# Attention in a two-layer encoder trunk: own tiles for the rotation, and another order of squares, evictions and rotations

## The chip, the cores and the metric

The kernel runs on one core of a Trainium2 chip. The metric is device time in microseconds (us). Every number below comes from the page of one profiled execution, from views of its trace, or from the run times.

Engines in the profile: PE (TensorE; PEld is its loading of weights), DVE (VectorE), ACT (ScalarE), POOL (GpSimd) and SP (SyncE, which issues nearly all DMAs). Each engine executes its own list of instructions in order, and waits at an instruction until the semaphores of other engines allow it.

## The reference

A trunk of two layers on 256 tokens of 1024 channels. Each layer is half a SwiGLU feed-forward block, a mixer, and another half block; the first mixer is a convolution module, the second is latent attention. All in float32. The change lies in the attention:

```python
def mla(h, positions, w_a, g_q, g_kv, w_uq, w_ukv, w_o):
    a = h @ w_a                                   # 512 query, 256 key/value, 64 rotary columns
    c_q = rmsnorm(a[..., :Q_LORA], g_q)
    c_kv = rmsnorm(a[..., Q_LORA:Q_LORA + KV_LORA], g_kv)
    k_rope = a[..., Q_LORA + KV_LORA:]
    q = jnp.einsum("bsc,chd->bshd", c_q, w_uq)    # 8 heads of 128 + 64
    q_nope, q_rope = q[..., :QK_NOPE], q[..., QK_NOPE:]
    kv = jnp.einsum("bsc,chd->bshd", c_kv, w_ukv)
    ...
    q_rope = apply_rope(q_rope, cos[:, :, None, :], sin[:, :, None, :])
    k_rope = apply_rope(k_rope, cos, sin)
    ...                                           # chunk-causal softmax, values, w_o
```

`h` is itself an rmsnorm of the stream, with gain `mix_norm`.

## The kernel before

**Splitting.** Float32 products are made of three passes (`mm3`, L267): both operands are split into a high part, rounded to the format that PE multiplies at full rate (`hi`, `Xh`, `CQh`), and a low part, the rest (`lo`, `Xl`, `CQl`). For weights, ACT casts the high part (L185) and DVE subtracts the low part (L186), each block of 128 x 2048 in two pieces of 1024. Blocks are loaded by SP into `raw` (3 buffers), their parts lie in `hi` and `lo` (5 buffers each). A `raw` buffer is free for the next load when its casts are done.

**Rows.** The 256 tokens are two row tiles of 128 (tb 0 and 1, the first and second rows).

**The stage around the change** (`mla_in`, L1104). For each row tile, `low` (L1124) makes the query product `a` (512 columns, weights wa 0 and 1) and then the key product `a` (320 columns, wa 2 and 3). `normed` (L1136) normalizes each: two squares on ACT with sums (`squares`, L293, each writes a scratch tile `junk` that nobody reads), sums and power -1/2 on POOL (`power`, L302), a product with the row's own factor `R[tb]` (L1139), and on DVE the scaled copy `cn` (L1141). The squares are scaled by `R[tb]`, so they need it too. `key_rope` (L1144) scales the 64 rotary key columns (`kx`) and rotates them twice (`rope`, L1085), into both halves of `kd`. PE then transposes `cn` (`tp`, L313), ACT evicts the high parts (L328) and DVE the low parts (L332), into `CQ` for queries and `CKh`, `CKl` for keys (`split_rows`, L321). The rotary queries `qr` (L1198) are the first product of `CQ`; each row tile is rotated on DVE into `qrope` (L1205). `nope` (L1180) makes the other queries and keys.

**The rotation** is three products and a sum on DVE: by the cosines (L1093), two halves by the sines (L1095), and their sum (L1097). The first product goes to `t1`, a tile of the pool `tmp` with tag "s", two buffers, which the scratch of the squares, `junk`, shares:

```python
        t1 = tmp.tile([P, 512], F32, tag="s", name=uid("rp1"))
        t2 = pool.tile([P, 512], F32, tag="rp", name=uid("rp2"), bufs=2)
```
```python
        junk = tmp.tile([P, 512], F32, tag="s", name=uid("junk"))
```

**The stream's own norm** (`Norm`, L356). The first rows are transposed by PE. The second rows of `h` go another way: DVE transposes blocks of 32, and two DMAs per half bring them to the right partitions (`turn_blocks`, L340, tiles `ht`, `hd`, `hb`). `end(q)` (L410) evicts half q of the second rows from `hb`: four `Xh` on ACT (L417), four `Xl` on DVE (L418), ordered behind the casts of the last loaded weight block. `late` (L424) does both halves and then `rms(1)`: the squares of `h` (ACT) and R of the second rows (POOL).

**What sets the order.** A scheduler orders each engine's list by priority and by its own estimate of times. Functions marked `urgent` (L191) get a high priority; `order(a, b)` (L135) puts a behind b; weight casts stand behind the last six urgent pieces of work of their engine (`behind`, L139). Before, in the first rows' key step, the whole of `X.late()` came ahead of the loads and the key norm:

```python
                if tb == 0 and i == 1:
                    X.late()
                    load_ahead(1)
```

Of the kernel before, what the change touches and what calls it, by code (L numbers as in the profile page):

```python
# [11 lines left out]
F32 = mybir.dt.float32  # L12
# [3 lines left out]
AF = mybir.ActivationFunctionType  # L16
ALU = mybir.AluOpType
AX = mybir.AxisListType

P = 128  # L20
# [11 lines left out]
H = 8  # L32
# [4 lines left out]
KVL = 256  # L37
# [25 lines left out]
GCOL = {}  # L63
# [19 lines left out]
def trunk(ctx: ExitStack, tc: tile.TileContext, x, xt, pos, invf, gains, gfin, wdw,  # L83
          f1w13, f1w2, f2w13, f2w2, cw1, cw2, wa, wuq, wukv, wo, wpair, out):
    nc = tc.nc
# [5 lines left out]
    tmp = ctx.enter_context(tc.tile_pool(name="tmp", bufs=2))  # L91
    small = ctx.enter_context(tc.tile_pool(name="small", bufs=4))
# [5 lines left out]
    def uid(s):  # L98
        n_uid[0] += 1
        return f"{s}_{n_uid[0]}"  # L100
# [29 lines left out]
    loaded = []  # L130
    n_used = [0]
# [3 lines left out]
    def order(ins, first):  # L135
        tc.add_manual_dep(ins.ins, first.name, mybir.DependencyInfo(
            mybir.DependencyClass.NoSync, mybir.DependencyReason.DATA), reason="order")
# [7 lines left out]
    casts = {}  # L145
# [140 lines left out]
    def rstd(src, n, name, scale_in=1.0, after=()):  # L286

        ss = small.tile([P, 2], F32, tag="ss", name=uid("ss"))
        for i in range(2):
            squares(ss, src, n, i, scale_in, after if i else ())  # L290
        return power(ss, n, name)

    def squares(ss, src, n, i, scale_in=1.0, after=()):  # L293
        nh = n // 2
        junk = tmp.tile([P, 512], F32, tag="s", name=uid("junk"))
        sq = nc.scalar.activation(junk[:, :nh], src[:, i * nh:(i + 1) * nh], AF.Square, scale=scale_in,  # L296
                                  accum_out=ss[:, i:i + 1])
        for a in after:
            order(sq, a.ins)
        return sq  # L300

    def power(ss, n, name):  # L302
        ms = small.tile([P, 2], F32, tag="ms", name=uid("ms"))
        nc.gpsimd.tensor_tensor(ms[:, 0:1], ss[:, 0:1], ss[:, 1:2], op=ALU.add)  # L304
        nc.gpsimd.tensor_scalar(ms[:, 1:2], ms[:, 0:1], 1.0 / n, EPS, op0=ALU.mult, op1=ALU.add)
        r = small.tile([P, 1], F32, tag="r", name=uid(name))
        nc.gpsimd.tensor_tensor(r, ms[:, 1:2], neghalf, op=ALU.pow)
        return r
# [11 lines left out]
    @urgent  # L320
    def split_rows(src, q, n, gcol, dh, dl, tb, after=(), low_after=(), turned=None,  # L321
                   lows=None):

        b = transposed(src, q, n, after, turned)
        for j in range(n):
            k = q + j
            g = G[:, gcol + k:gcol + k + 1]
            high = nc.scalar.activation(dh[:, k, tbs(tb)], b[:, j * P:(j + 1) * P], AF.Copy, scale=g)  # L328
        for j in range(n):
            k = q + j  # L330
            g = G[:, gcol + k:gcol + k + 1]
            low = nc.vector.scalar_tensor_tensor(dl[:, k, tbs(tb)], b[:, j * P:(j + 1) * P], g,  # L332
                                                 dh[:, k, tbs(tb)].bitcast(F32), op0=ALU.mult, op1=ALU.subtract)
            if lows is not None:
                lows.append(low)
            for a in low_after:
                order(low, a.ins)
        return high
# [17 lines left out]
    class Norm:  # L356


        def __init__(self, gname, half=False, turn_by_dma=None):
            self.col = GCOL[gname]  # L360
            self.half = half

            self.pool = turn_by_dma
            self.turning = []
            self.whole = False
            self.xh = xp.tile([P, KT, S], F32R, tag="Xh", name=uid("Xh"))
            self.xl = xp.tile([P, KT, S], F32R, tag="Xl", name=uid("Xl"))
            self.r = [None] * NT
            self.rh = [None] * NT
            self.turned = ()  # L370
            self.lows = []

            self.between = None

# [34 lines left out]
        @urgent  # L409
        def end(self, q):  # L410

            for j in range(4):
                k = 4 * q + j
                g = G[:, self.col + k:self.col + k + 1]
                t = self.turning[q][:, j]
                high, low = (x[:, k, tbs(1)].rearrange("p (i q) -> p i q", q=32) for x in (self.xh, self.xl))
                both = (nc.scalar.activation(high, t, AF.Copy, scale=g),  # L417
                        nc.vector.scalar_tensor_tensor(low, t, g, high.bitcast(F32), op0=ALU.mult, op1=ALU.subtract))  # L418

                for i in range(PIECES):  # L420
                    for ins, cast in zip(both, casts[len(loaded) - 1, i]):
                        order(ins, cast.ins)

        def late(self):  # L424

            if self.whole:
                return
            if self.pool:
                for q in range(2):
                    self.end(q)  # L430
            else:
                self.part(1, 1)
            self.rms(1)
# [648 lines left out]
        nc.scalar.activation(sn[:, :, 1, :], r3, AF.Sin)  # L1082
        return cc, sn

    def rope(pool, dst, src, n, cc, sn, tb):  # L1085

        w = n * 64
        t1 = tmp.tile([P, 512], F32, tag="s", name=uid("rp1"))
        t2 = pool.tile([P, 512], F32, tag="rp", name=uid("rp2"), bufs=2)
        a = t1[:, :w].rearrange("p (n i f) -> p n i f", i=2, f=32)  # L1090
        b = t2[:, :w].rearrange("p (n i f) -> p n i f", i=2, f=32)
        full = [P, n, 2, 32]
        nc.vector.tensor_tensor(a, src, cc[:, tb, :, :].unsqueeze(1).to_broadcast(full), op=ALU.mult)  # L1093
        for i in range(2):
            nc.vector.tensor_tensor(b[:, :, i, :], src[:, :, 1 - i, :],  # L1095
                                    sn[:, tb, i, :].unsqueeze(1).to_broadcast([P, n, 32]), op=ALU.mult)
        nc.vector.tensor_add(dst, t1[:, :w], t2[:, :w])  # L1097


# [4 lines left out]
    def mla_in(act, X, make_next, cc, sn):  # L1104
        R = X.r
        CQ = act.tile([P, H, S], F32R, tag="CQ", name="CQ")
        CQh, CQl = CQ[:, :4, :], CQ[:, 4:, :]
        CKh = act.tile([P, 2, S], F32R, tag="CKh", name="CKh")
        CKl = act.tile([P, 2, S], F32R, tag="CKl", name="CKl")
# [23 lines left out]
            return u  # L1133

        @urgent
        def normed(u, n, tb):  # L1136
            r2 = rstd(u[:, :n], n, "r2", scale_in=R[tb])
            rr = small.tile([P, 1], F32, tag="rr", name=uid("rr"))
            nc.gpsimd.tensor_tensor(rr, r2, R[tb], op=ALU.mult)  # L1139
            cn = act.tile([P, n], F32, tag=f"cn{n}", name=uid("cn"), bufs=2)  # L1140
            nc.vector.tensor_scalar(cn, u[:, :n], rr, None, op0=ALU.mult)  # L1141
            return cn

        def key_rope(u, tb):  # L1144
# [10 lines left out]
        cq, ck, kd = [], [], []  # L1155
        last = None
        for tb in range(NT):
            for i, w in enumerate((QL, KVL + ROPE)):
                u = low(parts[2 * i:2 * i + 2], w, tb, last)
                last = last_low[0]  # L1160
                if tb == 0 and i == 1:
                    X.late()
                    load_ahead(1)
                if i == 0:
                    cq.append(normed(u, QL, tb))
                    if tb == 1:
                        load_ahead()
                else:
                    ck.append(normed(u, KVL, tb))
                    kd.append(key_rope(u, tb))  # L1170
                if tb == 1 and i == 1:
                    split_rows(cq[0], 0, 4, GCOL["q"], CQh, CQl, 0)
# [22 lines left out]
        for tb in range(NT):  # L1195
            u = bank("A", "qr")
            for k in range(4):
                mm3(u, CQh[:, k, tbs(tb)], CQl[:, k, tbs(tb)], hi[:, k * 512:(k + 1) * 512],  # L1198
                    lo[:, k * 512:(k + 1) * 512], k == 0, k == 3)
            if tb == 0:  # L1200
                split_rows(cq[1], 0, 4, GCOL["q"], CQh, CQl, 1)
                for t in range(NT):
                    split_rows(ck[t], 0, 2, GCOL["kv"], CKh, CKl, t)
            q = act.tile([P, 512], F32, tag="cn512", name=uid("qrope"), bufs=2)
            rope(act, q, u.rearrange("p (n i f) -> p n i f", i=2, f=32), H, cc, sn, tb)  # L1205
            qr.append(q)
        part, = weights()
        nope(part, QN, 4, CQh, CQl, 512, 0, (0, 4))
        for t in range(NT):
            b = transposed(kd[t], 0, 1)  # L1210
# [3 lines left out]
        for tb in range(NT):  # L1214
            b = transposed(qr[tb], 0, 4)
# [4 lines left out]
        for tb in range(NT):  # L1220
            for d in range(2):
                b = bank("A", "v")
# [107 lines left out]
    X = mla(X, lambda act: Norm("ffn2_1", half=True, turn_by_dma=rows), cc, sn)  # L1330
# [96 lines left out]
```

## Time and profile before

| | |
|---|---|
| median of 3 runs | 933.79 us (932.66 to 934.49) |
| the profiled execution | 933.97 us, of which its span 932.2 us |
| mean granted clock of TensorE | 0.993 |
| SP's queue | 193.27 MB, 59.5% of 16 DMA engines' span |
| chain that ended last | PE 91%, DVE 4%, ACT 2%, DMA 1%, POOL 1%, issue 1% |

The profile's times count from the first instruction. A row of a timeline has start, duration, engine, line, operation, output and inputs, shapes and count, and in brackets the idle time before it with its releaser. A row of the waits has engine, line and tile, who was waited for, the total in us, the times and the longest. A row of the windows has, for each stretch, the busy time of PE, PEld, DVE, ACT and POOL, then the granted clock of TensorE, the DMA share and GB/s. The attention's preparation lies between 642 us, where PE starts `a`, and 698 us, where it starts the scores in earnest.

### The profile page before, as it was taken

Reading aid. Unit: us, or ns where it says so; the run is one execution under the profiler, and the core shown is the slowest. Engines: PE = TensorE matmul, PEld = TensorE weight load, DVE = VectorE, ACT = ScalarE, POOL = GpSimd, SP = SyncE. Lnnn points to the kernel's source line nnn. Section 1 sums busy time; section 2 is a strip of 40 time slices with the busy share of each in tenths; the row PEclk is TensorE's granted clock in tenths of the full one; section 3 lists DMA queues with packets and bytes.
Section 4 is the critical chain, followed back from the end, with each engine's and each line's share of the span. In section 5 each row is a group of like instructions: output and inputs, shape, how many; then the busy total and the mean of one; then the engine's idle time right before and its main releaser. Section 6 shows DMA issues by size and latency. Waiting matters only on the chain.

```text
span 932.2 us, 12108 instructions
## 1 busy us (share of the span) xinstructions
PE 914.9 (98%) x4346; PEld 767.0 (82%) x4346; DVE 590.1 (63%) x931; ACT 494.8 (53%) x844; POOL 123.4 (13%) x255
## 2 busy tenths in 40 slices
PE   9999999999999999999999999999699999999997
PEld 7888888898978888888888888888598888888886
DVE  5896664489987666564576656544745686656633
ACT  7664443488876544453455545434746584445421
POOL 1710000089940000000100000001200010000000
PEclk9999999999999999999999999999899999999999
DMA  9887775534227777775477777644541468767711
GB/s 339 311 313 231 288 248 197 181 137 169 89 80 258 249 248 239 237 261 181 165 256 255 249 253 248 223 147 150 197 150 46 181 238 279 249 231 239 253 46 46
DMA packets 65292, 194.73 MB, mean 209 GB/s; under 512 B 11856, under 2 KB 37072, under 8 KB 45904
## 3 DMA queue, kind: packets, MB, share of 16 engines
q1 hardware_dynamic: 64656, 193.27, 59.5%
q8 instruction: 34, 0.56, 0.2%
q10 hardware_dynamic: 576, 0.69, 0.2%
q14 instruction: 26, 0.21, 0.1%
HBM read 179.78 MB, written 14.16 MB: 208 GB/s over the span
## 4 chain that ended last, share of the span: by engine, by line
PE 91%; DVE 4%; ACT 2%; DMA 1%; POOL 1%; issue 1%; SPq 0%; POOLq 0%; ACTq 0%; DVEq 0%
PE u L272 17%; PE u L273 17%; PE u L269 17%; PE o L269 9%; PE o L272 9%; PE o L273 9%; DVE acc L820 3%; PE u L743 2%; PE gate L743 2%; PE o L984 1%; PE u L278 1%; PE tp L313 1%; PE nope L269 1%; PE nope L273 1%; PE nope L272 1%; PE sc L1236 1%
## 5 line engine op out<-in xcount | busy, mean ns | idle before, releaser
L186 DVE TENSOR_TENSOR lo<-raw,hi 128x1024 fp32r<-128x1024 f32 (+1 forms) x292 | 344.2, 1219 | 176.8 <-ACT hi L185 176.3
L185 ACT CAST hi<-raw 128x1024 fp32r<-128x1024 f32 x294 | 292.5, 1046 | 252.3 <-PE o L273 85.2
L269 PE MATMUL u<-lo,Xh 128*128 128x512 f32 x688 | 267.8, 389 | 0.0
L273 PE MATMUL u<-hi,Xl 128*128 128x512 f32 x688 | 267.8, 389 | 0.0
L272 PE MATMUL u<-hi,Xh 128*128 128x512 f32 x688 | 267.7, 389 | 0.0
L273 PEld LDWEIGHTS u<-hi,Xl 128*128 128x128 f32 x688 | 129.1, 188 | 27.2 <-DVE Xl L332 0.4
L269 PEld LDWEIGHTS u<-lo,Xh 128*128 128x128 f32 x688 | 129.1, 188 | 27.0
L272 PEld LDWEIGHTS u<-hi,Xh 128*128 128x128 f32 x688 | 129.1, 188 | 26.7
L272 PE MATMUL o<-hi,Gh 128*128 128x512 f32 (+1 forms) x356 | 137.9, 387 | 0.0
L273 PE MATMUL o<-hi,Gl 128*128 128x512 f32 (+1 forms) x356 | 137.8, 387 | 0.0
L269 PE MATMUL o<-lo,Gh 128*128 128x512 f32 (+1 forms) x356 | 137.2, 387 | 0.0
L304 POOL TENSOR_TENSOR ms<-ss 128x1 f32<-128x1 f32 x16 | 9.4, 587 | 608.9 <-ACT junk L296 608.9
L269 PEld LDWEIGHTS o<-lo,Gh 128*128 128x128 f32 x356 | 66.9, 188 | 13.6
L273 PEld LDWEIGHTS o<-hi,Gl 128*128 128x128 f32 x356 | 66.9, 188 | 13.5
L272 PEld LDWEIGHTS o<-hi,Gh 128*128 128x128 f32 x356 | 66.9, 188 | 13.4
L636 DVE TENSOR_TENSOR Gl<-gb,Gh 128x512 fp32r<-128x512 f32 (+1 forms) x48 | 31.2, 651 | 58.0 <-ACT Gh L635 57.8
L635 ACT CAST Gh<-gb 128x512 fp32r<-128x512 f32 (+1 forms) x48 | 28.0, 584 | 71.7 <-DMA gb<-gd 71.5
L820 DVE SCALAR_TENSOR_TENSOR acc<-V,dw,acc 128x128 f32<-128x128 f32 (+1 forms) x176 | 54.5, 392 | 0.0
L841 ACT ACTIVATE prod<-V,dw 128x128 f32<-128x128 f32 (+1 forms) x129 | 46.1, 415 | 2.0 <-POOL Y L842 1.0
L711 DVE TENSOR_TENSOR s<-s,u 128x512 f32<-128x512 f32 (+1 forms) x48 | 30.5, 635 | 8.8 <-PE u L273 8.8
L710 ACT ACTIVATE s<-u,R 128x512 f32<-128x512 f32 (+1 forms) x48 | 31.2, 650 | 5.1 <-PE u L273 4.0
L842 POOL TENSOR_TENSOR odd<-odd,prod 128x128 f32<-128x128 f32 (+1 forms) x62 | 33.2, 538 | 0.0
(213 smaller groups left out, 866.3 us busy)
## 6 DMA issues: line engine op xcount, KB each, us to landing
raw<-in_f2w SPq DMA_DIRECT2D x66, 1024.0 KB, 5.1
raw<-in_f1w SPq DMA_DIRECT2D x62, 1024.0 KB, 5.3
raw<-in_cw SPq DMA_DIRECT2D x12, 1024.0 KB, 4.7
gd<-gt SPq DMA_DIRECT2D x160, 64.0 KB, 3.4
gb<-gd SPq DMA_DIRECT2D x40, 256.0 KB, 4.8
raw<-in_wo SPq DMA_DIRECT2D x4, 1024.0 KB, 4.8
raw<-in_wuq SPq DMA_DIRECT2D x3, 1024.0 KB, 4.7
raw<-in_f1w SPq DMA_DIRECT2D x8, 256.0 KB, 4.8
```

Source lines behind the costliest of these rows:

```text
L185: casts[len(loaded), i] = (nc.scalar.copy(hi[:, c], raw[:, c]), low.tensor_sub(lo[:, c], raw[:, c], hi[:, c].bitcast(F32)))
L186: low.tensor_sub(lo[:, c], raw[:, c], hi[:, c].bitcast(F32)))
L269: mm = nc.tensor.matmul(o, ah, bl, start=start, stop=False)
L272: nc.tensor.matmul(o, ah, bh, start=False, stop=False)
L273: return nc.tensor.matmul(o, al, bh, start=False, stop=stop)
L636: nc.vector.tensor_sub(Gl[:, f, tbs(tb)].rearrange("p t (i q) -> p t i q", q=32), bv, gh.bitcast(F32))
L710: nc.scalar.activation(s[:, :w], u[0, tb][:, :w], AF.Silu, scale=X.r[tb])
L711: nc.vector.tensor_mul(s[:, :w], s[:, :w], u[0, tb][:, w:] if both else u[1, tb])
L743: mm = nc.tensor.matmul(u[:, t], w[:, c], X.x[:, k, t], start=(k == 0), stop=(k == KT - 1))
L820: dve_last.append(nc.vector.scalar_tensor_tensor(out if j == j1 - 1 else y, v, w, y, op0=ALU.mult, op1=ALU.add))
L841: prods_last.append(nc.scalar.activation(p, v, AF.Copy, scale=w))
L842: pool_last.append(nc.gpsimd.tensor_tensor(o, o, p, op=ALU.add))
```

## The change

Four edits, all in the attention's preparation:

- `rope` takes both its temporaries from the stage's own pool, in tiles of their own with four buffers for each width, instead of one from "s".
- In the first rows' key step, only half 0 of the second rows is evicted ahead of the load of the rotary weight. Half 1 and `rms(1)` come inside the key norm: behind the key squares, ahead of the key's power. The `Xh` evictions of half 1 are ordered behind the key squares, the first keys' `cn` behind the last `Xl`.
- The order in `end` refers to the last used weight block instead of the last loaded one.
- The low parts of the second rows' queries and of all keys are collected, and the three products of both query rotations are ordered behind them.

```diff
@@ class Norm
-            self.lows = []
+            self.lows, self.highs = [], []
...
-                both = (nc.scalar.activation(high, t, AF.Copy, scale=g),
+                both = self.ends = (nc.scalar.activation(high, t, AF.Copy, scale=g),
                         nc.vector.scalar_tensor_tensor(low, t, g, high.bitcast(F32), op0=ALU.mult, op1=ALU.subtract))
 
+                self.highs.append(both[0])
                 for i in range(PIECES):
-                    for ins, cast in zip(both, casts[len(loaded) - 1, i]):
+                    for ins, cast in zip(both, casts[n_used[0] - 1, i]):
                         order(ins, cast.ins)
 
-        def late(self):
+        def late(self, first=0):
...
-                for q in range(2):
+                for q in range(first, 2):
                     self.end(q)
@@ rope
-        t1 = tmp.tile([P, 512], F32, tag="s", name=uid("rp1"))
-        t2 = pool.tile([P, 512], F32, tag="rp", name=uid("rp2"), bufs=2)
+        t1, t2 = (pool.tile([P, w], F32, tag=f"rp{w}", name=uid("rp"), bufs=4) for _ in range(2))
...
+        for ins in turned:
+            for first in after:
+                order(ins, first.ins)
         nc.vector.tensor_add(dst, t1[:, :w], t2[:, :w])
@@ mla_in, normed
-        def normed(u, n, tb):
-            r2 = rstd(u[:, :n], n, "r2", scale_in=R[tb])
+        def normed(u, n, tb, between=None):
+            ss = small.tile([P, 2], F32, tag="ss", name=uid("ss"))
+            for i in range(2):
+                sq = squares(ss, u[:, :n], n, i, R[tb])
+            if between is not None:
+                between()
+                for high in X.highs[4:]:
+                    order(high, sq.ins)
+            r2 = power(ss, n, "r2")
...
-            nc.vector.tensor_scalar(cn, u[:, :n], rr, None, op0=ALU.mult)
+            scaled = nc.vector.tensor_scalar(cn, u[:, :n], rr, None, op0=ALU.mult)
+            if between is not None:
+                order(scaled, X.ends[1].ins)
@@ mla_in, the loop over row tiles
-                    X.late()
+                    X.end(0)
                     load_ahead(1)
...
-                    ck.append(normed(u, KVL, tb))
+                    if tb == 0:
+
+                        ck.append(normed(u, KVL, tb, lambda: X.late(1)))
+                    else:
+                        ck.append(normed(u, KVL, tb))
@@ mla_in, rotary queries
-                split_rows(cq[1], 0, 4, GCOL["q"], CQh, CQl, 1)
+                lows = []
+                split_rows(cq[1], 0, 4, GCOL["q"], CQh, CQl, 1, lows=lows)
                 for t in range(NT):
-                    split_rows(ck[t], 0, 2, GCOL["kv"], CKh, CKl, t)
+                    split_rows(ck[t], 0, 2, GCOL["kv"], CKh, CKl, t, lows=lows)
...
-            rope(act, q, u.rearrange("p (n i f) -> p n i f", i=2, f=32), H, cc, sn, tb)
+            rope(act, q, u.rearrange("p (n i f) -> p n i f", i=2, f=32), H, cc, sn, tb, lows)
```

More of the change, by code (lines that the diff above doesn't have):

```diff
@@ L1083, in rope_tables, with rope @@
         return cc, sn
-    def rope(pool, dst, src, n, cc, sn, tb):
+    def rope(pool, dst, src, n, cc, sn, tb, after=()):
         w = n * 64
-        t1 = tmp.tile([P, 512], F32, tag="s", name=uid("rp1"))
-        t2 = pool.tile([P, 512], F32, tag="rp", name=uid("rp2"), bufs=2)
+        t1, t2 = (pool.tile([P, w], F32, tag=f"rp{w}", name=uid("rp"), bufs=4) for _ in range(2))
         a = t1[:, :w].rearrange("p (n i f) -> p n i f", i=2, f=32)
@@ L1092, in rope @@
         full = [P, n, 2, 32]
-        nc.vector.tensor_tensor(a, src, cc[:, tb, :, :].unsqueeze(1).to_broadcast(full), op=ALU.mult)
+        turned = [nc.vector.tensor_tensor(a, src, cc[:, tb, :, :].unsqueeze(1).to_broadcast(full), op=ALU.mult)]
         for i in range(2):
-            nc.vector.tensor_tensor(b[:, :, i, :], src[:, :, 1 - i, :],
-                                    sn[:, tb, i, :].unsqueeze(1).to_broadcast([P, n, 32]), op=ALU.mult)
+            turned.append(nc.vector.tensor_tensor(b[:, :, i, :], src[:, :, 1 - i, :],
+                                                  sn[:, tb, i, :].unsqueeze(1).to_broadcast([P, n, 32]), op=ALU.mult))
+        for ins in turned:
+            for first in after:
+                order(ins, first.ins)
         nc.vector.tensor_add(dst, t1[:, :w], t2[:, :w])
```

## The prediction, as put on record before the changed kernel ran

> **What bounds the kernel now.** I read the page first, then the waits of PE, then each engine's timeline around its longest wait.
>
> ```profile
> span 932.2 us, 12108 instructions
> PE 914.9 (98%) x4346; PEld 767.0 (82%) x4346; DVE 590.1 (63%) x931; ACT 494.8 (53%) x844; POOL 123.4 (13%) x255
> PEclk9999999999999999999999999999899999999999
> PE tp L313 <- DVE cn L1141: 5.7, 2, 5.1
> PE tp L313 <- DVE CKl L332: 1.4, 1, 1.4
> PE qr L273 <- DVE CQ L332: 0.5, 1, 0.5
> ```
>
> PE is busy for all but 17.3 us of the span, and the only slice whose clock digit is not 9 is the 29th (653 to 676 us). The three waits quoted, 7.6 us together, lie in that slice, where the attention prepares its queries and keys. A change to this preparation can pay only by making these waits shorter, or by keeping the clock up behind them. PE through that stretch:
>
> ```profile
> 654.63 0.48 PE L273 MATMUL a<-hi,Xl 128*128 128x512 f32 x1
> 656.80 0.39 PE L273 MATMUL a<-hi,Xl 128*128 128x512 f32 x1
> 660.40 0.31 PE L273 MATMUL a<-hi,Xl 128*128 128x320 f32 x1
> 663.06 0.39 PE L273 MATMUL qr<-hi,CQ 128*128 128x512 f32 x1
> 664.01 0.88 PE L313 MATMUL tp<-ident,cn 128*128 128x128 f32 x6 [0.56 <-DVE cn L1141]
> 670.02 0.69 PE L313 MATMUL tp<-ident,cn 128*128 128x128 f32 x2 [5.13 <-DVE cn L1141]
> 673.94 0.80 PE L273 MATMUL qr<-hi,CQ 128*128 128x512 f32 x1 [0.46 <-DVE CQ L332]
> ```
>
> The columns are start, duration, engine, line, operation and tiles; the bracket is the idle time before, and its releaser. The second rows' query product ends at 657.19 (656.80 + 0.39), their key product at 660.71. Then PE lacks the second rows' normalized keys `cn` (transposed at 670.02) and the low parts of the normalized queries (673.94). Who made them late:
>
> ```profile
> 652.18 1.28 ACT L417 ACTIVATE Xh<-hb,G 128x128 fp32r<-128x128 f32 x4 [1.37 <-DMA hb<-hd]
> 653.37 1.98 ACT L185 CAST hi<-raw 128x1024 fp32r<-128x1024 f32 x2
> 655.95 1.12 ACT L328 ACTIVATE CQ<-tp,G 128x128 fp32r<-128x128 f32 x4
> 660.70 0.48 ACT L296 ACTIVATE junk<-a,R 128x256 f32<-128x256 f32 x1 [3.63 <-DVE kd L1097]
> 661.61 3.88 ACT L185 CAST hi<-raw 128x1024 fp32r<-128x1024 f32 x4
> 665.39 0.37 ACT L296 ACTIVATE junk<-a,R 128x128 f32<-128x128 f32 x1
> 660.37 0.35 DVE L1097 TENSOR_TENSOR kd<-rp,rp 128x64 f32<-128x64 f32 x2
> 663.21 0.75 DVE L1141 TENSOR_SCALAR cn<-a,rr 128x512 f32<-128x512 f32 x1 [2.49 <-POOL rr L1139]
> 663.88 4.62 DVE L186 TENSOR_TENSOR lo<-raw,hi 128x1024 fp32r<-128x1024 f32 x4
> 669.48 0.48 DVE L1141 TENSOR_SCALAR cn<-a,rr 128x256 f32<-128x256 f32 x1 [0.99 <-POOL rr L1139]
> 673.54 1.12 DVE L332 SCALAR_TENSOR_TENSOR CQ<-tp,G,CQ 128x128 fp32r<-128x128 f32 x4
> 666.28 1.14 POOL L304 TENSOR_TENSOR ms<-ss 128x1 f32<-128x1 f32 x1 [3.10 <-ACT junk L296]
> ```
>
> ACT had the second rows' query sums to square from 657.19 on, and stood idle 3.63 us, until 660.70. The releaser is DVE's sum at the end of the first rows' key rotation (L1097), with which the squares share no data: their scratch `junk` and the rotation's `rp1` are tiles of one tag, "s", with two buffers. All that follows stands in file behind the squares: ACT's four casts, the key squares (665.39), POOL's power (666.28), `cn` (669.48), PE (670.02), DVE's next casts, the low parts (673.54), PE (673.94).
>
> **The change, part by part.** *Tiles of their own.* No instruction comes or goes; the query squares' wait for DVE goes. What is late next for them: PE's product, POOL's factor R of the second rows, or ACT's own queue. How fast a matmul's end reaches ACT, and the rows for the other two:
>
> ```profile
> 680.14 0.39 PE L273 MATMUL qr<-hi,CQ 128*128 128x512 f32 x1
> 680.58 2.00 ACT L185 CAST hi<-raw 128x1024 fp32r<-128x1024 f32 x2 [6.53 <-PE qr L273]
> 649.49 0.63 ACT L296 ACTIVATE junk<-h 128x512 f32<-128x512 f32 x1
> 650.92 0.31 PE L273 MATMUL a<-hi,Xl 128*128 128x320 f32 x1
> 651.00 0.20 POOL L304 TENSOR_TENSOR ms<-ss 128x1 f32<-128x1 f32 x1
> 651.56 0.55 POOL L307 TENSOR_TENSOR R<-ms,neghalf 128x1 f32<-128x1 f32 x1
> 651.08 0.75 DVE L1141 TENSOR_SCALAR cn<-a,rr 128x512 f32<-128x512 f32 x1 [2.01 <-POOL rr L1139]
> 652.61 1.23 DVE L418 SCALAR_TENSOR_TENSOR Xl<-hb,G,Xh 128x128 fp32r<-128x128 f32 x4 [0.79 <-ACT Xh L417]
> ```
>
> The first two rows give 0.05 us (680.53 to 680.58), so PE allows 657.24.
>
> *Squares of the first keys ahead.* In the built order, ACT goes from the first query squares to the rotary weight's two casts, the first keys' squares, the `Xh` evictions, the two squares of `h`, and `CQ`. At 649.49 the casts start (before, the squares of `h` did). Casts and key squares took 2.58 us (653.37 to 655.95), so they end at 652.07; the key product is there at 651.23. The evictions wait for their DMA as before and start at 652.18, the squares of `h` at 653.37 and take twice 0.63, `CQ` runs from 654.6 to 655.8. ACT is free before 657.24.
>
> R of the second rows is now computed behind those squares of `h`. POOL does two sums, two scalings and the power: 0.28 us a step (651.00 to 651.56 is two), 4 x 0.28 + 0.55 = 1.67. From 654.75 that is 656.4, 0.8 us ahead of need. I take nothing for it. Above: were POOL shut out until DVE's `Xl` and `CQ` evictions are through (656.4, below), R would come at 658.1 and cost 0.9 us. Below: no gain, since PE's product ends last.
>
> DVE casts before it evicts `Xl`: `cn` ends at 651.83, two casts take 2.31 (half of 4.62), the first `Xl` starts near 654.1 and lands near 654.5 (a quarter of 1.23 or a little more); PE reads it at 654.63. That is almost no slack. I take 0, and 0.3 us, one eviction, as the upper end. The other three land 0.3 us apart and are read 0.7 us apart. `CQ` low parts follow to 656.4, ahead of the first keys' `cn`, which POOL's factor releases only near 657.4 (before: 658.06).
>
> *The sum.* The query squares go from 660.70 to 657.24: 3.46 us. From there the order on ACT, POOL and DVE is unchanged up to the `CQ` low parts, so each of the quoted rows moves by 3.46 where its other input is in time. Query `cn`: 659.75, casts on DVE: 660.42. The key squares: 661.93, behind their product at 660.71. POOL: 662.82, as far into DVE's casts as before. Key `cn`: 666.02. PE transposes at 666.56 and takes up `qr` at 670.48 instead of 673.94. One load has to move too:
>
> ```profile
> 649.91 7.25 SPq L177 DMA_DIRECT2D raw<-in_wukv  x2
> raw<-in_wukv SPq DMA_DIRECT2D x2, 1024.0 KB, 4.9
> 698.40 0.36 PE L269 MATMUL nope<-CQ,hi 128*128 128x256 f32 x1
> 677.63 0.68 DVE L1093 TENSOR_TENSOR rp<-qr,cc 128x512 f32<-128x512 f32 x1
> ```
>
> The second of the two loads left SP near 656.8, when DVE had cast the rotary weight and freed a buffer. With that cast done near 654.1 it lands near 659.0, and ACT reads it at 662.6. Nothing else stands on SP in between, and POOL's queue holds no DMA.
>
> *Rotated queries behind low parts.* DVE does three products of the first rotation ahead of the last query weight's casts instead of behind them. The casts and the sums of the second key rotation are queued behind; the casts serve the matmuls at 698.40, the sums a transposition that PE reaches only after 36 matmuls. Cost 0, and no gain, since PE's dense run covers both; without that cover it would be about 1.4 us (0.68 for the first product, about as much for the two halves).
>
> *The clock.* Rows of one microsecond; the column behind POOL's is the granted clock:
>
> ```profile
> 669.00:670.00 1.00, 0.00 (x0) 0.00 (x0) 0.52 (x2) 0.64 (x3) 0.37 (x2) 0.72 0.97 410
> 679.00:680.00 1.00, 1.00 (x5) 0.85 (x5) 0.69 (x1) 0.00 (x0) 0.00 (x0) 0.66 0.68 262
> 928.00:929.00 1.00, 0.00 (x0) 0.00 (x0) 0.47 (x2) 0.58 (x1) 0.00 (x0) 0.92 0.00 0
> ```
>
> The clock fell to half at 669.44 (0.72 = 0.44 + 0.56/2) and came back at 679.68. (It fell once more at 928.84, after the last matmul.) PE was fed without a break from 673.94, so 5.74 us of dense work ran at half speed: 2.87 us lost. Does it fall again? Between 664.2 and 670.48 PE has three transpositions and two `qr` matmuls, about 1.0 us of work in 6.3 us (16%); in the 6.0 us before the fall at 669.44 it had 0.88 (15%). By that share it falls again, and the return waits for a dense run as before: no gain, no loss. By the longest single gap it may not: 2.4 us (664.2 to 666.56) then, against 4.55 us before the fall at 669.44. I take the fall, by the nearest row, and keep 0 to 2.87 us.
>
> The Trainium skill, "TensorE: Matmul & The Clock Gate", sections "What's actually happening" and "Why this matters for your kernels", says that the clock is halved after an idle window of some 3.4 us, and advises against gaps above about 3 us. By that rule the 2.4 us gap leaves the clock up, which is the first rival. The trace agrees so far (5.13 us of idle halved it), but shows no gap of 2.4 us.
>
> The profiled execution took 933.97 us, 1.8 more than its span and 0.18 over the median of the three runs. 933.97 - 3.46 = 930.5 by it, 930.3 by the median; I say 930.4.
>
> **The rivals.** *The clock stays up* (0.34): the waits shrink as above and no half-speed stretch follows: 930.5 - 2.87 = 927.6. For it: every gap is half of the one that preceded the fall. Against it: the share of work.
>
> *R or `Xl` comes late* (0.05): a new wait replaces part of the old. 930.4 + 0.9 = 931.3. For it: POOL's 1.14 us at 666.28, beside DVE's casts, where 0.20 is its time alone. Against it: the evictions are a quarter as long as a cast. The Trainium skill, "SBUF — State Buffer", section "SBUF: two separate sides", has POOL blocked for a whole DVE instruction with two SBUF inputs; by it only `Xl`, done at 655.3, holds R up, and R still comes in time.
>
> *The change doesn't do what it says* (0.05): the query squares are held by something else until near 660. Then the time is 933.0 to 934.2, no difference.
>
> *The clock stays down* (0.04), the other side: PE's run after 670.48 is fed by DVE and ACT with less lead, small waits break it, and the clock doesn't come back. To be slower by 0.2% (1.9 us; 0.2% is also about what a measurement of this kernel can tell from no change) it must lose 3.46 + 2.87 + 1.9 = 8.2 us, that is, 16.5 us of dense work at half speed, until 687.0. Price at that point 935.8, then 0.5 us for each further us. Against it: before, it came back after 5.74 us.
>
> **How the numbers follow.** Forecast 0.52, the others 0.34, 0.05, 0.05, 0.04. The forecast's own spread is that of the three runs (932.66 to 934.49), moved by 3.46: 929.2 to 931.0, widened to 931.4 for the bounds of R and `Xl`. The clock that stays up gives 927.2 to 928.5. The range 927.1 to 931.6 leaves out little more than the last two. Faster (under 931.9): 0.52 + 0.34 + 0.05 = 0.91; the same 0.05; slower 0.04.
>
> **What would show it.** In the changed kernel's profile: the wait of ACT's `junk` for DVE's `kd` is gone, and the query squares start 0.1 us behind PE's product (if behind POOL, the second rival). PE's longest wait for `cn` falls from 5.13 to about 2.4 us. The granted clock around 664 to 680 decides between 930.4 and 927.6: 0.50 for some 5 us of dense `qr` and `nope`, or 1.00. A wait of PE for `Xl` near 654.6 would show the missing slack. The forecast is wrong if the squares start later than 658, or if the clock holds.

## The result, and the profile after

| | before | after |
|---|---|---|
| median | 934.49 us (932.66 to 937.2, 9 runs) | 930.77 us (929.55 to 933.13, 9 runs) |
| ratio | 1 | 0.9954, 95% interval 0.9937 to 0.9970 |
| profiled execution | 933.97 us, span 932.2 us | 931.24 us, span 929.4 us |

The change makes the kernel 3.7 us faster by these medians; 930.4 was forecast. Four of the nine runs before took 936.45 to 937.2 us. A second measurement on another chip (after_again below) gives medians of 933.98 and 930.70, 3.3 us apart, with a ratio of 0.9974. The page of the changed kernel, the lines that answer to those of before:

```profile
span 929.4 us, 12106 instructions
PE 915.6 (99%) x4346; PEld 767.7 (83%) x4346; DVE 589.8 (63%) x931; ACT 494.2 (53%) x844; POOL 123.6 (13%) x255
PEclk9999999999999999999999999999899999999999
```

The clock's 8 in the 29th slice is still there. The waits of PE in the changed kernel (total, times, longest):

```profile
PE tp L313 <- DVE cn L1151: 2.4, 1, 2.4
PE tp L313 <- DVE CKl L332: 1.9, 1, 1.9
...
PE qr L273 <- DVE CQ L332: 0.5, 1, 0.5
```

The wait for the second keys' `cn` fell from 5.1 to 2.4 us. (The one for `CKl` grew by 0.5 because PE did the work ahead of it at full clock, the transpositions in 0.44 us instead of 0.69; `qr` behind it is not later for it.) To compare two executions inside the attention, one offset has to go first. Where PE starts the attention's first product, before, and then in the changed kernel:

```profile
642.09 0.39 PE L269 MATMUL a<-lo,Xh 128*128 128x512 f32 x1
```
```profile
643.86 0.39 PE L269 MATMUL a<-lo,Xh 128*128 128x512 f32 x1
```

The change begins behind this point, and no engine's order ahead of it differs. The 1.77 us come from the start of the program (before, then after):

```profile
6.54 0.73 PE L278 MATMUL u<-lo,Xh 128*128 128x512 f32 x2
7.11 0.62 PE L278 MATMUL u<-hi,Xl 128*128 128x512 f32 x2
```
```profile
7.01 1.05 PE L278 MATMUL u<-lo,Xh 128*128 128x512 f32 x2
7.86 1.05 PE L278 MATMUL u<-hi,Xl 128*128 128x512 f32 x2
```

The same pair of matmuls took 1.05 us instead of 0.62: in this execution PE's clock rose later. The trace's first record of the full clock is at 10.09 us, before's at 3.84. A second profile of the changed kernel starts its first `a` at 642.01, so the offset isn't the change's. From here on I count times from the first `a`: "at 15.22" is 15.22 us behind it. The changed kernel's rows that answer to the prediction's:

```profile
655.36 0.39 PE L273 MATMUL a<-hi,Xl 128*128 128x512 f32 x1
658.57 0.39 PE L273 MATMUL a<-hi,Xl 128*128 128x512 f32 x1
668.32 0.44 PE L313 MATMUL tp<-ident,cn 128*128 128x128 f32 x2 [2.44 <-DVE cn L1151]
672.23 0.79 PE L273 MATMUL qr<-hi,CQ 128*128 128x512 f32 x1 [0.46 <-DVE CQ L332]
659.08 0.48 ACT L296 ACTIVATE junk<-a,R 128x256 f32<-128x256 f32 x1 [1.71 <-PE a L273]
663.79 0.36 ACT L296 ACTIVATE junk<-a,R 128x128 f32<-128x128 f32 x1
655.56 1.13 DVE L418 SCALAR_TENSOR_TENSOR Xl<-hb,G,Xh 128x128 fp32r<-128x128 f32 x4
661.76 0.75 DVE L1151 TENSOR_SCALAR cn<-a,rr 128x512 f32<-128x512 f32 x1 [1.13 <-POOL rr L1149]
667.77 0.48 DVE L1151 TENSOR_SCALAR cn<-a,rr 128x256 f32<-128x256 f32 x1 [0.71 <-POOL rr L1149]
657.52 0.55 POOL L307 TENSOR_TENSOR R<-ms,neghalf 128x1 f32<-128x1 f32 x1
664.66 0.20 POOL L304 TENSOR_TENSOR ms<-ss 128x1 f32<-128x1 f32 x1 [2.94 <-ACT junk L296]
662.43 4.63 DVE L186 TENSOR_TENSOR lo<-raw,hi 128x1024 fp32r<-128x1024 f32 x4
666.06 1.41 POOL L307 TENSOR_TENSOR r<-ms,neghalf 128x1 f32<-128x1 f32 x1
```

ACT's squares now wait for PE's product, 0.12 us behind its end (658.57 + 0.39), and no longer for DVE's `kd`. Windows of the changed kernel, with the granted clock as third number from the right:

```profile
668.00:669.00 1.00, 0.69 (x4) 0.47 (x4) 1.00 (x3) 0.24 (x2) 0.00 (x0) 0.93 1.03 426
669.00:675.00 6.00, 3.66 (x12) 2.66 (x12) 6.00 (x20) 2.93 (x6) 0.00 (x0) 0.50 0.89 343
675.00:676.00 1.00, 1.00 (x5) 0.81 (x5) 1.00 (x3) 0.00 (x0) 0.00 (x0) 0.65 0.00 0
```

The clock fell at 668.86 and came back at 675.70, after 6.84 us instead of 10.24.

Here is the measure used below, for each kernel's profiled execution: where PE starts its first `a`, when PE takes up `qr` again (the row of `qr` that waits for `CQ`; from `qr`'s third matmul in e9, where it waits no more), when the last `nope` matmul starts, and how long the clock was at half in between (read from windows, to 0.02 us). What follows the last `nope` takes 226.47 to 226.56 us in every kernel here, so all that differs lies in these columns.

| kernel | first `a` | `qr` at | last `nope` at | half clock | median us | ratio (95%) |
|---|---|---|---|---|---|---|
| before | 642.09 | 31.85 | 63.55 | 10.24 | 934.49 | 1 |
| after | 643.86 | 28.37 | 59.03 | 6.84 | 930.77 | 0.9954 (0.9937 to 0.9970) |
| after_again | 642.01 | 28.47 | 58.84 | 6.82 | 930.70 | 0.9974 (0.9963 to 0.9985) |
| e1_tiles | 645.18 | 29.21 | 60.26 | 6.84 | 931.39 | 0.9986 (0.9976 to 0.9997) |
| e3_order | 644.60 | 29.82 | 61.37 | 10.24 | 932.48 | 0.9993 (0.9984 to 1.0001) |
| e4_norot | 642.43 | 28.58 | 59.28 | 6.84 | 930.95 | 0.9973 (0.9962 to 0.9985) |
| e7_tiles_rot | 642.39 | 28.87 | 59.48 | 6.82 | 930.15 | 0.9964 (0.9952 to 0.9977) |
| e6_warm | 642.13 | 28.53 | 57.61 | 0 | 928.91 | 0.9951 (0.9938 to 0.9964) |
| e10_before_warm | 645.64 | 31.42 | 60.47 | 0 | 931.49 | 0.9978 (0.9966 to 0.9991) |
| e9_before_held | 642.28 | 26.95 | 58.15 | 6.82 | 929.63 | 0.9954 (0.9939 to 0.9969) |
| e5b_held | 643.41 | 24.61 | 53.72 | 0 | 924.91 | 0.9904 (0.9891 to 0.9917) |

Ratios are to the kernel before on the same chip. They are estimated over all runs and are not the quotients of the medians. The median before was 932.96 beside e1, e3, e4 and e7, 933.98 beside after_again, e5b and e6, and 932.77 beside e9 and e10. The first `a` moves by up to 3.6 us from one execution to another, for reasons ahead of the change (last section), and the medians hold that spread too. Parts of half a microsecond are therefore read from the two columns behind it. Two executions of the changed kernel agree there within 0.1 and 0.2 us.

### The profile page after: what moved, and what is told of

Same layout as the page of the kernel before. It is cut to its first block, busy times and chain, and to the rows that moved or that the text cites. A ratio compares the mean times of both kernels' runs of the same rounds, so it can differ in the third digit from the quotient of the medians.

```text
span 929.4 us, 12106 instructions
## 1 busy us (share of the span) xinstructions
PE 915.6 (99%) x4346; PEld 767.7 (83%) x4346; DVE 589.8 (63%) x931; ACT 494.2 (53%) x844; POOL 123.6 (13%) x255
## 4 chain that ended last, share of the span: by engine, by line
PE 93%; DVE 3%; ACT 2%; POOL 1%; issue 1%; DMA 0%; POOLq 0%; ACTq 0%
PE u L273 17%; PE u L272 17%; PE u L269 17%; PE o L272 9%; PE o L269 9%; PE o L273 9%; PE gate L744 2%; DVE acc L821 2%; PE u L744 2%; PE o L985 1%; PE u L278 1%; PE tp L313 1%; PE nope L269 1%; PE nope L273 1%; PE nope L272 1%; PE sc L1253 1%
## 5 line engine op out<-in xcount | busy, mean ns | idle before, releaser
L273 PEld LDWEIGHTS o<-hi,Gl 128*128 128x128 f32 x356 | 66.9, 188 | 13.4
L272 PEld LDWEIGHTS o<-hi,Gh 128*128 128x128 f32 x356 | 66.9, 188 | 13.4
L345 DVE STREAM_TRANSPOSE gt<-s 128x512 f32<-128x512 f32 (+1 forms) x48 | 32.0, 666 | 1.4
```

The costliest lines, as they stand in the source:

```text
L272: nc.tensor.matmul(o, ah, bh, start=False, stop=False)
L273: return nc.tensor.matmul(o, al, bh, start=False, stop=stop)
L345: nc.vector.transpose(t[:, :w], src.rearrange("p (t j q) -> p j t q", t=n, q=32))
```

## The experiments

**One part at a time.** Theory A: the shared scratch costs the 3.46 us, and the other edits keep DVE's queue from taking part of it back. Rivals: the tiles alone do it (B), the order alone does it (C).

*e1_tiles* is the kernel before, and only

```diff
-        t1 = tmp.tile([P, 512], F32, tag="s", name=uid("rp1"))
-        t2 = pool.tile([P, 512], F32, tag="rp", name=uid("rp2"), bufs=2)
+        t1, t2 = (pool.tile([P, w], F32, tag=f"rp{w}", name=uid("rp"), bufs=4) for _ in range(2))
```

> The kernel before with one part of the change: the two temporaries of every rotation in tiles of their own; the order edits are left out. Theory A (the squares of the second rows' queries waited only because their scratch shares a tag with the rotation's temporaries): ACT's wait for DVE's kd (3.63 us) is gone, and the squares start some 0.1 us behind PE's product. But the planner, freed of the shared buffer, now puts the first query rotation's three products ahead of the second rows' key cn on DVE, and its sum ahead of the low parts of CQ, and the first keys' cn still stands behind kd. So most of the 3.46 us goes to those: about 1.6 us are left, 932.9 beside 934.5 for the kernel before. Theory B (the tiles alone bring the whole gain, the order edits nothing): 931.0, PE's longest wait for cn 2.4 us. Theory C (the order of DVE and ACT is what counts, the shared scratch is no limit): no difference, 934.5, and the squares still start near 660.7.

Rows of e1_tiles:

```profile
660.40 0.48 ACT L296 ACTIVATE junk<-a,R 128x256 f32<-128x256 f32 x1 [0.53 <-PE a L273]
...
663.19 0.35 DVE L1096 TENSOR_TENSOR kd<-rp,rp 128x64 f32<-128x64 f32 x2
663.46 0.74 DVE L1140 TENSOR_SCALAR cn<-a,rr 128x512 f32<-128x512 f32 x1
668.66 0.68 DVE L1092 TENSOR_TENSOR rp<-qr,cc 128x512 f32<-128x512 f32 x1
669.26 0.74 DVE L1094 TENSOR_TENSOR rp<-qr,sn 128x256 f32<-128x256 f32 x2
670.02 0.48 DVE L1140 TENSOR_SCALAR cn<-a,rr 128x256 f32<-128x256 f32 x1
```

The squares start at 15.22 (660.40 - 645.18), exactly as in the changed kernel: the wait is gone with this edit alone, so C falls. But the query `cn` has no wait of its own any more; it stands right behind `kd`, at 18.28 instead of 17.90. Ahead of the key `cn` the scheduler now puts the first query rotation's products, 1.3 us, and `cn` comes at 24.84 instead of 23.91. `qr` gains 2.64 us, not 3.48: B falls too, and so does my 1.6 for A, which was 1 us too low. In the changed kernel DVE idles 0.7 us for POOL ahead of that `cn` anyway, which I had not set off against the rotation. The median, 931.39, lies nearer to B's 931.0 than to A's 932.9, but with a first `a` between 642 and 646 the times can't tell 0.8 us at `qr`: that B falls is read from the rows of one profile.

*e3_order* is the changed kernel with the two lines of `rope` undone.

> The changed kernel with the rotation's temporaries back in the shared tag; the two order edits stay. Theory A: the query squares of the second rows wait for DVE's kd again; kd itself is earlier than in the kernel before, by some 1.8 us, because the first keys are normalized with less in front of them. PE's wait for cn falls from 5.1 to some 3.3 us, and the time is about 932.7, 1.9 above the changed kernel. Theory B (the tiles alone bring the whole gain): no gain, 934.5, with the squares held until 660.7. Theory C (the order alone brings it): 930.8 as the changed kernel, and no wait for kd.

Row of e3_order:

```profile
661.18 0.47 ACT L296 ACTIVATE junk<-a,R 128x256 f32<-128x256 f32 x1 [3.08 <-DVE kd L1101]
```

The wait for `kd` is back. It ends at 16.58 (661.18 - 644.60) instead of before's 18.61, so the squares start 2.03 us earlier, and `qr` comes 2.03 us earlier. The order edits leave the false wait in place and bring its end forward. 2.64 and 2.03 are not to be added: both shorten one wait, and with both the end of PE's product is the limit, at 15.22. By its runs e3_order can't be told from the kernel before (ratio 0.9993, interval up to 1.0001); its gain is seen in the profile alone.

*e4_norot* is the changed kernel with `rope(..., tb)` instead of `rope(..., tb, lows)`. *e7_tiles_rot* is the changed kernel with `X.late()` whole ahead of `load_ahead(1)` again, and `normed` without `between`.

> The changed kernel without its third part: the rotated queries are no longer ordered behind the low parts. DVE then takes the first query rotation's three products (some 1.4 us) ahead of the second rows' key cn, and its sum ahead of the low parts of CQ. Theory A, as in the prediction (this part costs and gains nothing, cover on PE hides it): 930.8, as the changed kernel. Theory A2 (in the built order it keeps the rotation from giving part of the gain back): the low parts of CQ come some 0.9 us later, PE takes up qr 0.9 us later, 931.7.

> The changed kernel without its second part: the second rows' evictions stand whole ahead of the first keys' squares again, as in the kernel before. Theory A (tiles give the 3.46 us, this part only keeps DVE from giving some back): the squares of the second rows' queries start right behind PE's product, but the scaling of these queries is held on DVE behind the first keys' late cn and their rotation up to kd, until about 660.7 instead of 659.1 (in the time of the kernel before). About 2.5 us of gain are left: 932.0. Theory B (the tiles and the third part bring it all): 930.8. Theory C (the second part brings it all): 934.5.

Rows of e4_norot, and then of e7_tiles_rot:

```profile
665.39 0.68 DVE L1093 TENSOR_TENSOR rp<-qr,cc 128x512 f32<-128x512 f32 x1
665.99 0.74 DVE L1095 TENSOR_TENSOR rp<-qr,sn 128x256 f32<-128x256 f32 x2
666.65 0.47 DVE L1151 TENSOR_SCALAR cn<-a,rr 128x256 f32<-128x256 f32 x1
```
```profile
660.55 0.35 DVE L1100 TENSOR_TENSOR kd<-rp,rp 128x64 f32<-128x64 f32 x2
660.82 0.74 DVE L1151 TENSOR_SCALAR cn<-a,rr 128x512 f32<-128x512 f32 x1
```

Without the third part the rotation goes ahead of the key `cn` (24.22 instead of 23.91), and `qr` is 0.21 us later. Nearly all of it is hidden in DVE's wait for POOL; A holds here rather than A2. Without the second part the query `cn` again stands behind `kd`, at 18.43, and `qr` is 0.50 us later. I had expected 1.2 of e7: right in place, too high in size. The rows of e7 also show on what the key `cn` hangs. Its key squares start at 19.92, as early as in the changed kernel (19.93). But DVE's four casts, which stand behind the query `cn`, end at 23.72 instead of 23.20 (662.43 + 4.63 - 643.86). POOL's power step beside them takes 1.41 us in both kernels (0.55 at 660.91 in the changed kernel, where DVE is idle), and ends 0.4 us behind the casts. So ahead of the key `cn` DVE's casts come last, by way of POOL, and not ACT's. The medians of e4 and e7 can't be told from the changed kernel's.

**Is the clock's fall worth what was worked out?** Two kernels keep PE busy in its gaps with matmuls whose results nobody uses; everything else is as in the changed kernel (*e6_warm*) or as before (*e10_before_warm*):

```diff
+                filled = [keep_warm(20, after=turned[-1])]    # e10: 44; behind the first keys' transpositions
...
+                    mm = keep_warm(16, after=mm)              # e10: 12; behind the second qr matmul
```

> The changed kernel with 20 and 16 more matmuls (bf16, 256 columns, results never used) in the two idle gaps of PE, between the first and second keys' transpositions and behind the second qr matmul of the second rows. They add no data dependency; they only keep PE busy where it waits. Theory S (the clock falls by PE's share of work over a stretch of some 3.4 us, and its fall costs half of the dense work done until it returns): the granted clock stays 1.00 from 660 to 680, and the time is 1.7 us below the changed kernel where its clock stays down 3.5 us of dense work, up to 2.6 where it stays longer: about 928.5 to 929.1. Theory G (the clock's fall costs nothing, PE's dense run after it is followed by slack): 930.8. If the added matmuls themselves run late and hold the real ones, up to 1 us slower.

> The kernel before with 44 and 12 more matmuls (bf16, 256 columns, results never used) in PE's two idle gaps, between the first and the second keys' transpositions and behind the second qr matmul of the second rows. Nothing else waits for them. If the clock falls by PE's share of work and the fall costs half of the dense work until it returns, as the prediction worked out (5.74 us at half speed, 2.87 lost): the granted clock stays 1.00 from 660 to 680, the last nope matmul comes 60.7 us behind the first product of the attention instead of 63.55, and the time is 931.1 beside 934. If the lost time is not on the path, 934. If the added matmuls hold the real ones, no gain or slower.

The stretch from 661 to 680 us in e6_warm and in e10_before_warm (it was 0.82 in the changed kernel, 0.73 before):

```profile
661.00:680.00 19.00, 17.67 (x127) 15.31 (x127) 18.02 (x36) 12.04 (x25) 2.99 (x4) 1.00 0.61 222
```
```profile
661.00:680.00 19.00, 17.18 (x121) 14.45 (x120) 15.33 (x41) 11.99 (x26) 4.20 (x9) 1.00 0.60 219
```

The clock stays at 1.00, and the last `nope` comes at 57.61 instead of 59.03 or 58.84, and at 60.47 instead of 63.55. Some 0.4 us of the 3.1 before is already there when `qr` is taken up (31.42 against 31.85), none in the changed kernel (28.53 against 28.37 and 28.47). Counted from `qr` to the last `nope`, the fall cost 2.65 us before and 1.3 to 1.6 in the two executions of the changed kernel. Half of the dense work until the clock's return gives 2.87, and 1.39 and 1.74: what is regained is the dense work behind the gap, as the prediction had it. Work that computes nothing makes the kernel some 1.8 us faster than the changed one, by medians on one chip (928.91 and 930.70).

**What is left of the wait.** Between the query squares and the key squares of the second rows, ACT and DVE still cast two blocks of weights (3.9 and 4.6 us). *e5b_held* is the changed kernel with fewer of them there, *e9_before_held* the same edit on the kernel before:

```diff
                     if tb == 1:
-                        load_ahead()
+                        load_ahead(2)
...
-        (hi, lo), = weights()
+        (hi, lo), = weights(more=False)
...
+                load_ahead()          # behind the split_rows of the keys
```

> The changed kernel, with the conversion of the two blocks of wukv (four casts each on ACT and DVE) held behind the low parts of CQ and CK instead of standing between the query squares and the key squares of the second rows; the loads keep their place. If what is left of PE's wait for the second rows' keys is the chain behind those casts (ACT's 3.9 us and DVE's 4.6 us of casts ahead of key squares and key cn), PE's 2.4 us and 1.9 us waits nearly go, qr is taken up about 5 us earlier, the clock stays up, and the time is 924 to 927. If instead the casts are only moved to where PE needs them (nope waits for its weights behind the low parts), the gain is given back: 930 or more, with PE waiting for hi or lo of wukv some 30 us later.

> The kernel before, without any part of the change, with the second block of wukv converted behind the low parts of CQ and CK (as in e5b_held) instead of ahead of the second rows' key squares. Theory A (two faults in one chain: the shared scratch holds the query squares until DVE's kd, and behind them the casts hold the key squares): the squares still start at 660.7 in the time of the kernel before, 18.6 us behind the first product of the attention; the casts between them and the key squares are 2 us shorter, so the second rows' keys are transposed some 3 to 4 us earlier than in the kernel before and qr is taken up again some 3.5 us earlier; with the clock kept up by the shorter gap up to 2.9 us more: 928 to 931 beside 934. It is then 3 to 4 us slower than e5b_held, and what the change is worth stays 3.5 us behind either choice. Theory D (with the casts held, nothing of the change is needed): 925, as e5b_held.

My text said that both blocks between the squares were wukv's and would move. In the built order the first is wuq's, for `nope`, and keeps its place; the second, the first of wukv, goes behind the low parts. PE's waits in e5b_held, and its windows over the same stretch:

```profile
PE tp L313 <- DVE CKl L332: 0.8, 1, 0.8
...
PE tp L313 <- DVE cn L1151: 0.5, 1, 0.5
```
```profile
661.00:680.00 19.00, 17.61 (x121) 15.83 (x121) 17.55 (x36) 13.86 (x29) 2.25 (x5) 1.00 0.46 160
```

`qr` is taken up 3.8 us earlier than in the changed kernel (some 5 were expected), the clock stays up with no matmul added, and PE doesn't wait for the moved block later. 924.91 us, ratio 0.9904: this beats both kernels. Row of e9_before_held:

```profile
660.54 0.48 ACT L296 ACTIVATE junk<-a,R 128x256 f32<-128x256 f32 x1 [3.61 <-DVE kd L1097]
```

The squares wait as before (at 18.26; before 18.61), but what stands behind them is shorter: `qr` at 26.95, 929.63 us, as good as the change by itself. D falls: on top of the held casts the change still brings 2.3 us at `qr` (3.5 were expected), and 4.4 at the last `nope`, because only in e5b_held's profile does the clock stay up.

**The same kernel again.**

> The changed kernel once more, as the measure for the runs beside it and for what differs between two executions of one program. Expected 930.8, within 929.5 to 933.2. Theory P (the offset of 1.77 us at the first product of the attention is the start of the program, where the clock rises at a moment that differs from execution to execution on a grid of about 3.4 us): the start offset differs again, and the distances inside the attention stay: query squares 13.4 us behind the first a product. Theory Q (the offset belongs to the changed kernel): 1.77 us again.

The first `a` came at 642.01, the query squares at 15.22 again (657.23). P holds, Q falls. (The 13.4 in the expectation looks like a slip: it is 657.24, forecast in before's time, less the changed kernel's first `a` at 643.86.)

## Why the prediction was right, point by point

| step | predicted, from before's first `a` | measured in after |
|---|---|---|
| query squares | 15.15 | 15.22 |
| query `cn` | 17.66 | 17.90 |
| key squares | 19.84 | 19.93 |
| POOL's sum of the keys | 20.73 | 20.80 |
| key `cn` | 23.93 | 23.91 |
| PE transposes | 24.47 | 24.46 |
| PE takes up `qr` | 28.39 | 28.37 |

- *Tiles of their own, and the sum.* Right: 3.48 us where 3.46 was forecast. That it fits to 0.02 is luck in part: the query `cn` and DVE's casts came 0.24 us later than forecast, and the key `cn` followed the casts' end after 0.71 us instead of 0.98, because POOL's last power step began ahead of that end and not behind it. What the prediction credited to the tiles alone is shared, though. By themselves they bring 2.64 (e1_tiles); "from there the order is unchanged" held only because the other two edits keep DVE's list in that order. The prediction read this from the built order of the whole change, and could not have carried it over to a part.
- *Squares of the first keys ahead.* Cost 0, as taken. R's power starts at 13.66 and ends at 14.21 (657.52 + 0.55), 1.0 us ahead of need; forecast 14.3. `Xl` starts at 11.70 (forecast 12.0) and PE reads it with no wait. The second rival (R or `Xl` late) did not come about. The edit is worth 0.50 us (e7_tiles_rot), for which the prediction had no term.
- *Rotated queries behind low parts.* Cost 0 and no gain forecast; worth 0.21 us (e4_norot).
- *The clock.* That it falls again was right, and the first rival was wrong: with 2.44 us as the longest gap it fell. The mis-sized term, in these two executions, is the dense work until its return. The prediction left it at 5.74 us; it was 3.47 (672.23 to 675.70), 1.74 us lost instead of 2.87. So the stage ends 4.52 us earlier instead of 3.46. But that extra 1.06 us can't be credited to the change. The clock falls and rises on a grid that lies elsewhere in each execution (last section), and in after_again 2.78 us of dense work ran at half speed. As an estimate, I laid that grid at every phase over PE's rows of both kernels, with a fall behind windows of under 1.55 us of work and a return behind those of 2.92 or more: in either kernel 2.4 to 5.8 us of dense work then run at half speed, 4.1 on average. The half clock lasts a step less in the changed kernel because the gap is shorter, not because less dense work is slow. By this estimate "no gain, no loss" holds on average, and before's profile showed an unlucky phase.
- *Why the total still fitted.* In the profiles, -4.52 of the stage and +1.77 of the start are -2.75, against 931.24 - 933.97 = -2.73. The medians moved by 3.72. The forecast of 930.4 lies 0.4 below 930.77, within the spread that the start alone makes; the 1.06 us of the clock can't be seen in the medians, nor in the second pair of medians (3.3 us).
- The rival of no change and the slower one did not come about: the squares started at PE's end, and the clock came back in the dense run.

## What to carry to other kernels

Look at which wait ends last on the idle engine, and whether the releaser shares data with it: a scratch tile in a common tag can put one engine behind another that it has nothing to do with. When such a wait goes, ask what the scheduler then puts into the freed queue, and build the parts one by one; here a quarter of the gain hung on two orderings. Then look at what is left in the same chain: weight casts that are needed late stood between two steps that were needed early, and holding half of them back on top of the change brought more (930.70 to 924.91 us) than the change itself.

## What the runs showed of the hardware

**The clock is decided on a fixed grid.** In each execution all the moments at which the clock fell or rose lie a multiple of 3.413 us apart, within 0.02: before 669.44, 679.68 and 928.84 (3 and 73 steps), in the changed kernel 668.86, 675.70 and 924.86 (2 and 73). Where the grid lies differs by execution. Windows on the grid, before and then in the changed kernel (the second number is PE's busy time):

```profile
662.62:666.03 3.41, 1.71 (x10) 1.00 (x8) 2.82 (x3) 3.41 (x8) 0.47 (x2) 1.00 0.00 0
666.03:669.44 3.41, 0.00 (x0) 0.00 (x0) 2.46 (x3) 3.41 (x10) 2.92 (x4) 1.00 0.60 195
669.44:672.86 3.42, 1.54 (x4) 0.82 (x4) 3.38 (x6) 2.31 (x5) 0.01 (x1) 0.50 1.00 419
672.86:676.27 3.41, 2.81 (x9) 2.23 (x10) 3.41 (x15) 0.91 (x3) 0.00 (x0) 0.50 0.80 286
676.27:679.68 3.41, 3.41 (x14) 3.02 (x14) 3.38 (x8) 0.00 (x0) 0.00 (x0) 0.50 0.37 91
```
```profile
665.46:668.87 3.41, 0.97 (x8) 0.65 (x6) 2.70 (x5) 2.65 (x9) 2.12 (x3) 1.00 0.87 310
668.87:672.28 3.41, 1.07 (x4) 0.23 (x2) 3.41 (x12) 3.00 (x6) 0.00 (x0) 0.50 0.92 329
672.28:675.70 3.42, 3.42 (x11) 3.03 (x12) 3.42 (x9) 0.06 (x1) 0.00 (x0) 0.50 0.68 285
```

PE's share decides, not its longest gap, as far as these windows show: around the attention, a fall followed each window with up to 1.30 us of work (e4_norot), and none followed one with 1.71 (before) or 2.02 (e5b_held); at its start e3_order fell after one with 1.46, and at its end the changed kernel after one with 1.51, e7_tiles_rot not after one with 1.59. The longest gap inside a window doesn't part them: e1_tiles fell after one with 1.17 us of work and a longest gap of 1.19, and not after the one ahead of it, with 2.19 and 1.22. Behind the attention's gap the return followed windows with 2.96 us of work or more, and none with 2.88 (e9_before_held) or less. The row of 2.96, of after_again:

```profile
669.84:673.26 3.42, 2.96 (x11) 2.50 (x11) 3.42 (x13) 0.52 (x2) 0.00 (x0) 0.50 0.90 309
```

This bound is rough: at the program's start the clock rose behind 2.80 (before) and not behind 2.92 (in the changed kernel). Before, the gap's end cut into one window more (2.81), which didn't bring the clock back: so the half clock lasted 3.4 us less in the changed kernel. The Trainium skill, "TensorE: Matmul & The Clock Gate", section "What's actually happening", has a free-running window of 3413 ns, and the grid agrees with that to the digit. But its rule there that the clock falls after an idle window, and its advice (section "Why this matters for your kernels") against gaps of over about 3 us, are too mild by these runs: a window 28% busy (0.97 of 3.41), with no gap above 2.44 us, halved the clock.

**A fall of the clock elsewhere.** With the grid at some phases the clock also falls near 252 us, in another stage that has many small matmuls. Three executions here show it. Their clock first rose at 5.76, 6.23 and 6.74 us; in the six whose first rise came at 3.84 to 5.57 and held, it didn't fall there. A row of e1_tiles:

```profile
252.00:262.00 10.00, 10.00 (x37) 8.86 (x36) 8.96 (x34) 7.83 (x28) 8.16 (x19) 0.50 0.31 106
```

There and in e10_before_warm it stayed down for 10.24 us, in e5b_held for 3.42, and the first `a` came at 645.18, 645.64 and 643.41 instead of 642.0 to 642.4. PE counts as busy in the window before the fall (the profile models the ends of matmuls), so it can't be read from the busy time; why it falls there stays open. This fall and the late rises at the start move the first `a` by up to 3.6 us (642.01 to 645.64) from one execution to another.

**The clock column starts at 1.00.** In the changed kernel's first 10 us the column shows 1.00 while pairs of matmuls take 1.05 us instead of 0.62; it knows of no state ahead of the first recorded transition, at 10.09 us. There the durations are to be read.
